# Output projection of a hybrid S5 / HGRN2 layer: sample tokens unsplit on array strips, blocks of every eighth token, two heads split in place, new order lists

## The chip, the cores and the metric

The program runs on one core of one Trainium2 chip. The metric is the device time of one execution in microseconds, as the median of several runs. TensorE (PE) multiplies into PSUM, VectorE (DVE) and ScalarE (ACT) do the elementwise work, GpSimd (POOL) a little of it, and SyncE (SP) issues nearly all DMAs.

## The reference

One layer, 1024 prompt tokens and 32 sample tokens (8 sequences of 4) with states from before. Cut to its core:

```python
h = rmsnorm(x, norm_g); proj = h @ w_in                  # (1056, 1024) @ (1024, 3072)
u, z_s, q, gf, iv, z_h = split(proj, 512 each)
y = S5(u)                                                # 32 groups, complex diagonal state of 64, scan over tokens
g = gelu(y); s5_out = g * sigmoid(g @ w_glu + b_glu) * silu(z_s)
f = lb + (1 - lb) * sigmoid(gf); k = (1 - lb) * sigmoid(-gf)
o = HGRN2(q, k, iv, log f)                               # 4 heads, S_t = diag(f_t) S + k_t v_t', o_t = S_t' q_t
hg_out = rmsnorm_per_head(o) * onorm_g * silu(z_h)
out = concat(s5_out, hg_out) @ w_out                     # (1056, 1024) @ (1024, 1024)
y = rmsnorm(x + out, final_norm_g)                       # also returned: all new states
```

## The kernel before

Every large product is made in float32r from operands split into a high and a low half, as three products: high x high, high x low, low x high. A split is a ScalarE copy (high) and a VectorE subtraction (low). Products of plain f32 tiles run as two records each in the trace.

*Start* (lines 123 to 329): x arrives in tiles of 128 tokens; x_norm takes mean squares (ScalarE, and VectorE for the pairs in DVE_SQ), the root (L172), and scales the tiles (L177, on GpSimd for the pairs in POOL_X, else on VectorE); x_split transposes on TensorE (L188) and splits. Three input projections (L199, tile iu) run as the token chunks come.

*S5 stage* (S5_ORDER): p prepares, m runs the scans of, an eighth of the groups; u, v and z are projections. *Head stage* (H_ORDER): per head f and q are projections, c is the chunkwise recurrence of the 1024 prompt tokens (head_c, two halves), s the sample tokens, n the norm, z the gate's projection, o the transposition and gating (head_out, into tile zh, stored to h_dram); g is an eighth of the GLU, stored to s_dram.

*Output stage* (OUT_ORDER, L990 to L1082): load_a brings one of the eight factors kt (0 to 3 from s_dram, 4 to 7 from h_dram, heads 0 to 3) through a raw buffer, of which there are three, and splits it into ah and al (L1014, L52); factors 0 to 3 are reordered into token order in that pass. load_o does the same for w_out. The 32 sample tokens are split into xs (high and low, 64 columns). Then nine token blocks, the sample block fourth: each takes 2 PSUM banks (the last block three parts) in turn out of eight and accumulates over the factors in the order of OUT_ORDER (L1053; the sample block L1057, two products). Each part is then added to the residual, squared, and the block normalised and stored.

The order lists give the order in which steps are written down and with it their priority; the scheduler of the framework places instructions on each engine's queue by priority and readiness, and the queue then runs in order. Steps under prio() rank above others; issue_after(i) keeps a step behind instruction i on its engine. DMAs that SP issues wait in its queue in order too.

## Time and profile before

| | |
|---|---|
| time, median of 3 runs | 542.88 us (542.69 to 543.5) |
| profiled execution: time, span | 542.94 us, 541.1 us |
| mean granted TensorE clock | 0.993 |
| busy: TensorE, VectorE, ScalarE, GpSimd | 514.6, 386.9, 313.7, 23.7 us |
| share of TensorE in the chain that ended last | 81% |

A row of a timeline gives the start, the time until the end of the group, the engine, the line and the tile names (written <- read). A matmul's duration includes its way through the array; the step from one start to the next is what a stream of them costs. "[2.10 <-ACT KT L805]" says that the engine stood idle for 2.10 us before it and that ScalarE's write of KT ended that.

### The profile page before, as it was taken

The numbers are of one execution on the slowest core, as the hardware profiler recorded it, in microseconds if no ns is written. First come the engines' busy times: TensorE is split into PE (matmuls) and PEld (weight loads), VectorE is DVE, ScalarE is ACT, GpSimd is POOL, SyncE is SP. The second block draws the span as 40 slices with busy tenths as digits, with TensorE's granted clock in tenths as the row PEclk, the third lists the DMA queues.
The fourth block names the chain that finished last, engine by engine and source line by source line (L and its number), as shares of the span: only waits on it lengthen the run. The fifth ranks groups of instructions, "written<-read, shape, count | busy, mean of one in ns | idle before, by whom it ended". The sixth has DMA issues, their size and how long they took to land.

```text
span 541.1 us, 11361 instructions
## 1 busy us (share of the span) xinstructions
PE 514.6 (95%) x4232; PEld 474.4 (88%) x4232; DVE 386.9 (71%) x1075; ACT 313.7 (58%) x877; POOL 23.7 (4%) x79
## 2 busy tenths in 40 slices
PE   2999999999999999999999999999999699999995
PEld 1999999999999999999999999999988577778885
DVE  5897849999989885996569637983699654375233
ACT  5957425645745659553984379835996577333112
POOL 0471000000000100000000000000000000000000
PEclk9999999999999999999999999999999989999999
DMA  8800922341434217333232306343255527535312
GB/s 310 267 20 14 281 59 82 94 150 30 143 130 151 70 64 225 101 102 84 70 95 82 122 9 176 106 122 121 78 149 171 190 84 235 179 125 168 116 40 78
DMA packets 52631, 66.19 MB, mean 122 GB/s; under 512 B 3680, under 2 KB 34272, under 8 KB 52576
## 3 DMA queue, kind: packets, MB, share of 16 engines
q1 hardware_dynamic: 52432, 65.21, 38.0%
q8 instruction: 33, 0.54, 0.4%
q10 hardware_dynamic: 144, 0.26, 0.1%
q14 instruction: 22, 0.18, 0.1%
HBM read 46.43 MB, written 19.02 MB: 121 GB/s over the span
## 4 chain that ended last, share of the span: by engine, by line
PE 81%; ACT 7%; DVE 5%; DMA 3%; issue 2%; SPq 0%; ACTq 0%; DVEq 0%
PE ip L199 32%; PE op L1053 15%; PE vp L253 9%; PE iu L199 7%; PE glu L972 3%; PE xt L188 2%; PE y L572 2%; DMA or<-in_w_out_dram 2%; PE b L516 1%; PE y L574 1%; PE kv L810 1%; DVE Qv L52 1%; DMA wr_b<-in_w_in_dram 1%; ACT S L888 1%; PE po L816 1%
## 5 line engine op out<-in xcount | busy, mean ns | idle before, releaser
L199 PE MATMUL ip<-xh,wl_b 128*128 128x384 f32 (+1 forms) x408 | 133.9, 328 | 0.0
L199 PE MATMUL ip<-xh,wh_b 128*128 128x384 f32 (+1 forms) x408 | 132.9, 326 | 1.0 <-ACT sg L976 0.7
L199 PE MATMUL ip<-xl,wh_b 128*128 128x384 f32 (+1 forms) x408 | 133.3, 327 | 0.0
L199 PEld LDWEIGHTS ip<-xh,wh_b 128*128 128x128 f32 x408 | 76.6, 188 | 1.9 <-ACT sg L976 1.1
L199 PEld LDWEIGHTS ip<-xh,wl_b 128*128 128x128 f32 x408 | 76.9, 188 | 1.0 <-issue 0.6
L199 PEld LDWEIGHTS ip<-xl,wh_b 128*128 128x128 f32 x408 | 76.8, 188 | 0.7 <-issue 0.6
L1053 PE MATMUL op<-oh,ah 128*128 128x512 f32 (+1 forms) x136 | 52.8, 388 | 1.7 <-ACT ah L1014 1.0
L1053 PE MATMUL op<-ol,ah 128*128 128x512 f32 (+1 forms) x136 | 52.1, 383 | 0.0
L1053 PE MATMUL op<-oh,al 128*128 128x512 f32 (+1 forms) x136 | 49.6, 380 | 0.0
L253 PE MATMUL vp<-wh_v,xh 128*128 128x256 f32 x128 | 37.0, 289 | 0.0
L253 PE MATMUL vp<-wh_v,xl 128*128 128x256 f32 x128 | 36.3, 284 | 0.0
L253 PE MATMUL vp<-wl_v,xh 128*128 128x256 f32 x128 | 36.3, 284 | 0.0
L1063 ACT ACTIVATE rsq<-res 128x512 f32<-128x512 f32 (+2 forms) x19 | 11.5, 606 | 39.6 <-DVE res L52 38.6
L104 ACT ACTIVATE wh_b<-wr_b 128x512 fp32r<-128x512 f32 x40 | 24.4, 630 | 15.8 <-DMA wr_b<-in_w_in_dram 11.0
L1053 PEld LDWEIGHTS op<-oh,ah 128*128 128x128 f32 x136 | 26.0, 191 | 7.4 <-ACT ah L1014 1.3
L52 DVE TENSOR_TENSOR res<-op,res 128x512 f32<-128x512 f32 (+2 forms) x19 | 12.3, 660 | 27.2 <-PE op L1053 25.0
L52 DVE TENSOR_TENSOR wl_b<-wr_b,wh_b 128x512 fp32r<-128x512 f32 x40 | 27.3, 684 | 5.5 <-ACT wh_b L104 5.4
L1053 PEld LDWEIGHTS op<-ol,ah 128*128 128x128 f32 x136 | 26.0, 191 | 5.1
L1053 PEld LDWEIGHTS op<-oh,al 128*128 128x128 f32 x136 | 25.7, 190 | 5.2
L199 PE MATMUL iu<-xl,wh_b 128*128 128x256 f32 (+2 forms) x72 | 24.9, 350 | 0.0
L253 PEld LDWEIGHTS vp<-wh_v,xh 128*128 128x128 f32 x128 | 24.2, 189 | 0.4 <-issue 0.4
L253 PEld LDWEIGHTS vp<-wh_v,xl 128*128 128x128 f32 x128 | 24.2, 189 | 0.0
(314 smaller groups left out, 1277.9 us busy)
## 6 DMA issues: line engine op xcount, KB each, us to landing
wr_b<-in_w_in_dram SPq DMA_DIRECT2D x40, 256.0 KB
gr<-y_dram SPq DMA_DIRECT2D x16, 272.0 KB
or<-in_w_out_dram SPq DMA_DIRECT2D x16, 256.0 KB
res<-in_x_p_dram SPq DMA_DIRECT2D x8, 512.0 KB
out_dram<-res SPq DMA_DIRECT2D x7, 512.0 KB
u_dram<-uT SPq DMA_DIRECT2D x4, 576.0 KB
U<-u_dram SPq DMA_DIRECT2D x8, 288.0 KB
y_dram<-Y SPq DMA_DIRECT2D x8, 272.0 KB
```

The costliest lines, as they stand in the source:

```text
L52: eng.tensor_tensor(out=out, in0=a, in1=b, op=op)
L104: S.activation(h, raw, AF.Copy)
L188: PE.transpose(ps[:, n * 128 - n0 : n * 128 - n0 + m], xrs[n][kt // 4][:, kt % 4 * 128 : kt % 4 * 128 + 128], ident[:m, :m])
L199: PE.matmul(ps[:, :nn], a[:, kt * 128 : (kt + 1) * 128], b[kt][:, n0 : n0 + nn], start=(kt == 0 and i == 0), stop=(kt == KT - 1 and i == 2))
L253: PE.matmul(ps[:, :256], a[kt][:, tok], b, start=(kt == 0 and i == 0), stop=(kt == KT - 1 and i == 2))
L516: PE.matmul(ps[:, i * 136 : (i + 1) * 136], W[:, g0 + i, :], U[:, g0 + i, 0:136], start=True, stop=True)
L572: PE.matmul(ps[:, i * 136 : (i + 1) * 136], T[:, g0 + i, :], U[:, g0 + i, 8:144], start=True, stop=False)
L574: PE.matmul(ps[:, i * 136 : (i + 1) * 136], CA[:, g0 + i, 1:9, :].rearrange("p n c -> p (n c)"), SS[:, g0 + i, :], start=False, stop=True)
L810: PE.matmul(pkv[:, sl], KT_[:, sl], v[:, 4 * hb + i, :], start=True, stop=True)
L972: PE.matmul(ps[:, :272], a[:, kt, mo * 128 : mo * 128 + 128], b[:, kt, :], start=(kt == 0 and i == 0), stop=(kt == 3 and i == 2))
L1053: PE.matmul(ps, a[kt][:, tok], b[kt][:, cs], start=(ik == 0 and i == 0), stop=(ik == KT - 1 and i == 2))
L1063: S.activation(sq[:m, cs], r[:m, cs], AF.Square, accum_out=ss[:m, ip : ip + 1])
```

## The change

The 32 sample tokens of the output projection are no longer split: plain f32 products with 32 stationary columns each go to four 32-column strips of the array, four factors at a time, with w_out loaded once more, unsplit; the four partial sums are added on the way out of PSUM, and they are made after blocks 2 and 4. A block of 128 prompt tokens now takes every eighth token, so that factors 0 to 3 are split in the order in which they are stored, while the weights of factors 4 to 7 are read with a step of eight. Heads 2 and 3 are split from their tile zh, with no way through h_dram. In head_c four psC products per group become three. x_norm(0) is written down ahead of the first weights, whose casts go behind its root. Fewer squares go to VectorE and fewer multiplies to GpSimd. fng is loaded after OUT_ORDER into a tile of its own. The output blocks use six banks in turn. The last part's square sums on VectorE, and its scaling is cut in three. The order lists are new. The diff, cut (the old final loop's removed lines are in the listing above):

```diff
-S5_ORDER = "p0 p1 p2 m0 m1 v0 p3 u3 p4 m2 m3 v1 m4 p5 p6 m5 p7 z1 m6 z2 m7 z0 z3"
-
-
-H_ORDER = "f0 q0 c0 s0 g0 z0 g1 f1 q1 c1 n0 s1 g2 o0 z2 f2 n1 g3 q2 c2 g4 z1 s2 n2 o1 g5 f3 g6 q3 c3 s3 o2 n3 g7 z3 o3"
-
-OUT_ORDER = "a0 w5 a1 w1 w0 w2 w4 w3 a5 a3 a4 a2 w6 a6 w7 a7"
+S5_ORDER = "p0 p1 p2 m0 m1 v0 p3 u3 p4 m2 m3 v1 m4 p5 p6 p7 m5 m6 z0 z2 z1 m7 z3"
+H_ORDER = "f0 q0 g0 c0 s0 n0 z0 g1 f1 q1 c1 g2 o0 z2 f2 s1 g4 q2 n1 g3 c2 z1 s2 g5 f3 g6 q3 c3 n2 s3 n3 o2 o1 g7 z3 o3"
+OUT_ORDER = "w5 a1 w2 w0 w1 a0 w4 w3 a5 a3 a4 a2 w6 a6 w7 a7"
 PRIO = 10000
 
-DVE_SQ = {(n, 1) for n in range(5)}
-POOL_X = {(n, 1) for n in range(2, 9)}
+DVE_SQ = {(0, 1), (1, 1)}
+POOL_X = {(n, 1) for n in (5, 6, 7, 8)}
...
             SY.dma_start(raw, src[:, i * 512 : (i + 1) * 512])
-            with prio():
+            with prio(), tc.issue_after(xrs["root"].ins) if name == "b0" else nullcontext():
                 S.activation(h, raw, AF.Copy)
                 tt(V, l, raw, h.bitcast(F32), SUB)
...
-    xs = cp.tile([128, KT, 64], F32R, name="xs")
+    st = cp.tile([128, KT, 32], F32, name="st")
...
         xspare = lambda name: un(name, 576)
+        x_norm(0)
         w0 = load_w(io["w_in"][0], "b0")
...
-                q4 = Qv.rearrange("p (s i e x) -> p s i e x", i=4, e=2, x=hh)
+                last = hh == 32
+                q4 = Qv.rearrange("p (s i e x) -> p s i e x", i=4, e=3 if last else 2, x=hh)
...
-                tt(V, q4[:, :, 0, 1, :], q4[:, :, 3, 0, :], M.unsqueeze(2).to_broadcast([128, ns, hh]), MUL)
+                tt(V, q4[:, :, 1, 2, :] if last else q4[:, :, 0, 1, :], q4[:, :, 3, 0, :], M.unsqueeze(2).to_broadcast([128, ns, hh]), MUL)
...
-                Qn = ht(f"Qv{4 * hh}", 512 if last else 1024)
+                Qn = ht(f"Qv{4 * hh}", 512 if last else 1536 if hh == 8 else 1024)
...
-                q = Q32[:, 256 * n : 256 * n + 256]
+                q = Q32[:, 384 * n : 384 * n + 384]
                 o = 96 * n
-                ks = [K32[:, 128 * n + 32 * j : 128 * n + 32 * j + 32] for j in range(3)]
-                PE.matmul(psC[0:32, o : o + 64], ks[0], q[:, 64:128], start=True, stop=True)
-                PE.matmul(psC[32:64, o : o + 96], ks[1], q[:, 96:192], start=True, stop=True)
-                PE.matmul(psC[64:96, o : o + 96], ks[2], q[:, 128:224], start=True, stop=True)
-                PE.matmul(psC[0:32, o + 64 : o + 96], ks[0], q[:, 32:64], start=True, stop=True)
+                for j, b in enumerate((q[:, 96:192], q[:, 160:256],
+                                       q[:, 96:384].rearrange("p (i x) -> p i x", x=96)[:, :, 0:32])):
+                    PE.matmul(psC[32 * j : 32 * j + 32, o : o + 96],
+                              K32[:, 128 * n + 32 * j : 128 * n + 32 * j + 32], b, start=True, stop=True)
...
-        SY.dma_start(h_dram[h], zg)
+        if h < 2:
+            SY.dma_start(h_dram[h], zg)
...
-    fng = zp.tile([128, NT], F32, name="fng", tag="z", bufs=2)[:, :D]
-    SY.dma_start(fng, io["fng"])
+    fng = fp.tile([128, D], F32, name="fng", bufs=1)
     ahi, alo, ohi, olo = {}, {}, {}, {}
     early = [(wp, "whi", 3, wp, "wlo", 3)] * 2 + [(zp, "v", 4, zp, "v", 4)]
-    st = xs
     def load_a(kt):
         pa, ta, na, pb, tb, nb = early.pop(0) if early else (fp, "a", 10, fp, "a", 10)
         a = pa.tile([128, NP], F32R, name=f"ah{kt}", tag=ta, bufs=na)
         b = pb.tile([128, NP], F32R, name=f"al{kt}", tag=tb, bufs=nb)
-        av = a.rearrange("p (c j) -> p c j", j=8)
-        bv = b.rearrange("p (c j) -> p c j", j=8)
         for i in range(2):
-            src = rawt(f"ar{kt}{i}")
+            half = slice(512 * i, 512 * i + 512)
+            at, bt = a[:, half], b[:, half]
             if kt < 4:
+                src = rawt(f"ar{kt}{i}")
                 SY.dma_start(src, s_dram[kt][:, 544 * i : 544 * i + 544])
                 sj = src.rearrange("p (j t) -> p j t", t=136)
-                pv, qv = sj[:, :, :128].transpose([0, 2, 1]), sj[:, :, 128:].transpose([0, 2, 1])
-                at, bt = av[:, :, 4 * i : 4 * i + 4], bv[:, :, 4 * i : 4 * i + 4]
-                last = i == 0
+                pv, qv = sj[:, :, :128], sj[:, :, 128:].transpose([0, 2, 1])
+                at, bt = (t.rearrange("p (j t) -> p j t", t=128) for t in (at, bt))
+                short = i == 0
             else:
                 n = (512, 544)[i]
-                SY.dma_start(src[:, :n], h_dram[kt - 4][:, 512 * i : 512 * i + n])
-                pv = src[:, :512].rearrange("p (c j) -> p c j", j=8)
-                qv = src[:, 512:544].rearrange("p (c j) -> p c j", j=4)
-                at, bt = av[:, 64 * i : 64 * i + 64], bv[:, 64 * i : 64 * i + 64]
-                last = i == 1
+                if kt < 6:
+                    src = rawt(f"ar{kt}{i}")
+                    SY.dma_start(src[:, :n], h_dram[kt - 4][:, 512 * i : 512 * i + n])
+                else:
+                    src = zgs[kt - 4][:, 512 * i : 512 * i + n]
+                pv = src[:, :512]
+                qv = src[:, 512:n].rearrange("p (c j) -> p c j", j=4)
+                short = i == 1
             S.activation(at, pv, AF.Copy)
             tt(V, bt, pv, at.bitcast(F32), SUB)
-            if last:
-                sh = st[:, kt, 0:32].rearrange("p (c j) -> p c j", j=4)
-                sl = st[:, kt, 32:64].rearrange("p (c j) -> p c j", j=4)
-                S.activation(sh, qv, AF.Copy)
-                tt(V, sl, qv, sh.bitcast(F32), SUB)
+            if short:
+                S.copy(st[:, kt].rearrange("p (c j) -> p c j", j=4), qv)
         ahi[kt], alo[kt] = a, b
+    def tokens(a, kt, n):
+        return a[kt][:, 128 * n : 128 * n + 128] if kt < 4 else a[kt].rearrange("p (c j) -> p j c", j=8)[:, n]
+    def rows(t, n):
+        return t.rearrange("(c j) d -> j c d", j=8)[n]
     def load_o(kt):
         oh = xp.tile([128, NT], F32R, name=f"oh{kt}", tag="x")
...
         for i in range(2):
             cs = slice(512 * i, 512 * i + 512)
             raw = rawt(f"or{kt}{i}")[:, :512]
-            SY.dma_start(raw, io["w_out"][kt][:, cs])
+            xrs["o"] = SY.dma_start(raw, io["w_out"][kt][:, cs])
             S.activation(oh[:, cs], raw, AF.Copy)
             tt(V, ol[:, cs], raw, oh[:, cs].bitcast(F32), SUB)
         ohi[kt], olo[kt] = oh, ol
+    def finish(n, r, sq, ss, ip, cs, parts):
+        m = 128 if n < 8 else 32
+        if n == 7 and ip == 2:
+            V.scalar_tensor_tensor(out=sq[:, cs], in0=r[:, cs], scalar=1.0, in1=r[:, cs], op0=MUL, op1=MUL,
+                                   accum_out=ss[:, 2:3])
+            S.activation(ss[:, 2:3], ss[:, 2:3], AF.Sqrt, bias=ss[:, 3:4], scale=1.0 / D)
+            V.reciprocal(ss[:, 2:3], ss[:, 2:3])
+            S.activation(sq[:, 384:768], r[:, 384:768], AF.Copy, scale=ss[:, 2:3])
+            V.scalar_tensor_tensor(out=sq[:, cs], in0=r[:, cs], scalar=ss[:, 2:3], in1=fng[:, cs], op0=MUL, op1=MUL)
+            V.tensor_scalar(sq[:, 0:384], r[:, 0:384], ss[:, 2:3], None, op0=MUL)
+            SY.dma_start(rows(io["y_p"], n)[:, 0:384], sq[:, 0:384])
+            S.dma_start(rows(io["y_p"], n)[:, 384:D], sq[:, 384:D])
+            return
+        S.activation(sq[:m, cs], r[:m, cs], AF.Square, accum_out=ss[:m, ip : ip + 1])
+        if n == 7:
+            tt(V, r[:, cs], r[:, cs], fng[:, cs], MUL)
+        if ip == 1:
+            tt(V, ss[:m, 0:1], ss[:m, 0:1], ss[:m, 1:2], ADD)
+            V.tensor_scalar(ss[:m, 3:4], ss[:m, 0:1], 1.0 / D, EPS, op0=MUL, op1=ADD)
+        if ip == parts - 1:
+            S.activation(ss[:m, 0:1], ss[:m, 3:4], AF.Sqrt)
+            V.reciprocal(ss[:m, 0:1], ss[:m, 0:1])
+            V.scalar_tensor_tensor(out=r[:m], in0=r[:m], scalar=ss[:m, 0:1], in1=fng[:m], op0=MUL, op1=MUL)
+            SY.dma_start(rows(io["y_p"], n) if n < 8 else io["y_s"], r[:m])
+    def row(n):
+        m = 128 if n < 8 else 32
+        r = fp.tile([128, D], F32, name=f"res{n}", tag="res", bufs=3)
+        SY.dma_start(r[:m], rows(io["x_p"], n) if n < 8 else io["x_s"])
+        sq = fp.tile([128, D], F32, name=f"rsq{n}", tag="rsq", bufs=2)
+        return r, sq, fp.tile([128, 4], F32, name=f"fs{n}", tag="fs", bufs=2)
     emit(OUT_ORDER, {"a": load_a, "w": load_o})
+    SY.dma_start(fng, io["fng"])
     ks = [int(i[1:]) for i in OUT_ORDER.split() if i[0] == "a"]
-    banks, it = (mmt, mmt, mmt, ppt, axt, axt, byt, byt), 0
...
+    banks, it = (mmt, mmt, mmt, axt, axt, byt), 0
+    wfull = [p.tile([128, n], F32, name=f"ws{j}", tag=t, bufs=b)[:, :D]
+            for j, (p, n, t, b) in enumerate(((wp, D, "whi", 3), (wp, D, "wlo", 3), (zp, 1152, "o", 2), (zp, 1152, "o", 2)))]
+    short = []
+    def short_load(i):
+        for j in range(4):
+            SY.dma_start(wfull[j], io["w_out"][ks[4 * i + j]])
+    def short_mms(i):
+        if i == 0:
+            short.extend((ppt("os0"), byt("os1")))
+        for c in range(2):
+            for j in range(4):
+                PE.matmul(short[c][32 * j : 32 * j + 32, :], st[:, ks[4 * i + j], :], wfull[j][:, 512 * c : 512 * c + 512],
+                          start=(i == 0), stop=(i == 1))
+    for n in range(8):
+        r, sq, ss = row(n)
+        parts = ((0, 512), (512, 256), (768, 256)) if n == 7 else ((0, 512), (512, 512))
         for ip, (c0, cn) in enumerate(parts):
             ps = banks[it](f"op{n}{ip}")[:, :cn]
             it = (it + 1) % len(banks)
             cs = slice(c0, c0 + cn)
             for ik, kt in enumerate(ks):
...
+                for i, (a, b) in enumerate(((ahi, ohi), (ahi, olo), (alo, ohi))):
+                    PE.matmul(ps, tokens(a, kt, n), b[kt][:, cs], start=(ik == 0 and i == 0),
+                              stop=(ik == KT - 1 and i == 2))
+            tt(V, r[:, cs], ps, r[:, cs], ADD)
+            finish(n, r, sq, ss, ip, cs, len(parts))
+        if n == 0:
+            with tc.issue_after(xrs["o"].ins):
+                short_load(0)
+        if n == 2:
+            short_mms(0)
+            short_load(1)
+        if n == 4:
+            short_mms(1)
+            r, sq, ss = row(8)
+            for c in range(2):
+                cs = slice(512 * c, 512 * c + 512)
+                tt(V, r[:32, cs], short[c][0:32], r[:32, cs], ADD)
+                for j in range(1, 4):
+                    S.copy(sq[:32, cs], short[c][32 * j : 32 * j + 32])
+                    tt(V, r[:32, cs], r[:32, cs], sq[:32, cs], ADD)
+                finish(8, r, sq, ss, c, cs, 2)
```

## Rows read from the trace of the kernel before

**Rows 1.** The page: busy time, share of the span and instructions by engine.
```profile
PE 514.6 (95%) x4232; PEld 474.4 (88%) x4232; DVE 386.9 (71%) x1075; ACT 313.7 (58%) x877; POOL 23.7 (4%) x79
```

**Rows 2.** Windows: length, busy time of each engine, granted clock, DMA share, GB/s.
```profile
13.50:27.00 13.50, 13.50 (x97) 13.50 (x96) 10.91 (x25) 13.11 (x36) 5.59 (x7) 1.00 0.81 269
397.00:423.00 26.00, 23.92 (x312) 20.84 (x312) 24.92 (x74) 18.64 (x50) 0.00 (x0) 1.00 0.46 151
423.00:441.00 18.00, 13.61 (x127) 11.06 (x127) 10.50 (x31) 10.57 (x32) 0.00 (x0) 0.81 0.50 156
441.00:453.00 12.00, 10.71 (x62) 7.35 (x63) 3.19 (x6) 11.59 (x35) 0.00 (x0) 1.00 0.53 177
```

**Rows 3.** Waits of TensorE: us in total, times, longest.
```profile
PE xt L188 <- DVE xr L177: 10.0, 1, 10.0
...
PE kt L803 <- DVE C L791: 1.5, 1, 1.5
...
PE op L1053 <- ACT ah L1014: 1.0, 1, 1.0
```

**Rows 4.** Timeline of the start: start us, us, engine, line, tile, shape [idle before].
```profile
6.60 0.15 DVE L170 SCALAR_TENSOR_TENSOR rstd<-ss_x 128x2 f32<-128x2 f32 x1
...
8.02 0.19 ACT L172 ACTIVATE rstd<-rstd 128x2 f32<-128x2 f32 x1
...
8.76 0.16 DVE L173 RECIPROCAL rstd<-rstd 128x2 f32<-128x2 f32 x1
...
9.42 1.67 DVE L177 TENSOR_SCALAR xr<-xr,rstd 128x512 f32<-128x512 f32 x4
...
15.47 5.11 POOL L177 TENSOR_SCALAR xr<-xr,rstd 128x512 f32<-128x512 f32 x3 [13.79 <-DVE rstd L173]
```

**Rows 5.** Chain pieces (start, us, what), then two timeline rows of TensorE.
```profile
243.82 0.89 PE kv L810 x8
...
265.47 0.57 PE oS L880 x16
...
445.43 0.39 PE L1057 MATMUL op<-ol,xs 128*64 128x512 f32 x1
...
448.66 0.40 PE L1057 MATMUL op<-ol,xs 128*64 128x512 f32 x1
```

**Rows 6.** Timeline of TensorE: first and last of one sC group.
```profile
427.88 0.24 PE L771 MATMUL sC<-Qv,K 128*32 128x64 f32 x1 [0.49 <-ACT o L823]
...
428.54 0.23 PE L774 MATMUL sC<-Qv,K 128*32 128x32 f32 x2
```

**Rows 7.** Output passage: durations (min/median/max ns), timelines, a wait of SP, chain.
```profile
L1014 ACT ACTIVATE ah<-ar x16: 614/841/1212, 396.4 to 473.5; 128x512 fp32r<-128x512 f32 x16
...
L52 DVE TENSOR_TENSOR al<-ar,ah x16: 680/860/1143, 397.6 to 474.2; 128x512 fp32r<-128x512 f32 x16
...
396.43 1.14 ACT L1014 ACTIVATE ah<-ar 128x512 fp32r<-128x512 f32 x1
...
426.07 1.28 ACT L1030 ACTIVATE oh<-or 128x512 fp32r<-128x512 f32 x2 [4.19 <-DMA or<-in_w_out_dram]
...
SPq L989 <- DMA h_dram<-zh: 2.8, 1, 2.8
...
433.04 2.08 PE L810 MATMUL kv<-v,KT 128*128 128x128 f32 x8 [2.10 <-ACT KT L805]
...
435.11 3.35 PE op L1053 x9
```

**Rows 8.** Weight loads of two lines: ns min/median/max, first and last start, shape.
```profile
L1053 PEld LDWEIGHTS op<-oh,ah x136: 186/188/333, 418.8 to 534.8; 128*128 128x128 f32 x136
...
L880 PEld LDWEIGHTS oS<-S,Qm x64: 106/110/110, 265.4 to 441.5; 128*32 128x32 f32 x64
```

**Rows 9.** Timeline of the close.
```profile
535.44 0.42 DVE L52 TENSOR_TENSOR res<-op,res 128x256 f32<-128x256 f32 x1 [1.16 <-PE op L1053]
...
537.73 0.37 ACTq L1077 DMA_DIRECT2D out_dram<-rsq  x1
```

More of the change, by code (lines that the diff above doesn't have):

```diff
@@ L1 @@
 import math
-from contextlib import ExitStack
+from contextlib import ExitStack, nullcontext
 import concourse.bass as bass
@@ L1037, in hybrid_layer @@
-    for n in (0, 1, 2, 8, 3, 4, 5, 6, 7):
-        m = 128 if n < 8 else 32
-        tok = slice(n * 128, n * 128 + 128)
-        r = fp.tile([128, D], F32, name=f"res{n}", tag="res", bufs=3)
-        SY.dma_start(r[:m], io["x_p"][tok] if n < 8 else io["x_s"])
-        sq = fp.tile([128, D], F32, name=f"rsq{n}", tag="rsq", bufs=2)
-        ss = fp.tile([128, 4], F32, name=f"fs{n}", tag="fs", bufs=2)
-        last = n == 7
-        parts = ((0, 512), (512, 256), (768, 256)) if last else ((0, 512), (512, 512))
+    banks, it = (mmt, mmt, mmt, axt, axt, byt), 0
@@ L1050, in hybrid_layer @@
             for ik, kt in enumerate(ks):
-                if n < 8:
-                    for i, (a, b) in enumerate(((ahi, ohi), (ahi, olo), (alo, ohi))):
-                        PE.matmul(ps, a[kt][:, tok], b[kt][:, cs], start=(ik == 0 and i == 0),
-                                  stop=(ik == KT - 1 and i == 2))
-                else:
-                    for i, b in enumerate((ohi, olo)):
-                        PE.matmul(ps[:64], st[:, kt, :], b[kt][:, cs], start=(ik == 0 and i == 0),
-                                  stop=(ik == KT - 1 and i == 1))
```

30 lines of the change are left out of this document (3 added, 27 removed).

## The prediction

> **What bounds the kernel now.** I read the page's engine table first, then the busy time by stretch, then what TensorE waited for, and last the timelines of the stretches in which it waited. TensorE is busy for 514.6 of 541.1 us [rows 1], so 26.5 us are left in which no matmul is under way. Three places hold most of it: the first 10.0 us until the first transposition has a normalised x tile [rows 3]; the stretch from 397 to 453 us, where the three windows leave 2.1, 4.4 and 1.3 us, 7.8 together [rows 2]; and the close after the last matmul, from about 535.4 to 541.1, 5.7 us [rows 9]. That leaves 3.0 us for everything else. So a change pays if it takes TensorE work out, or shortens one of these three; work taken from another engine pays only inside them. The middle stretch costs more than its idle time: in 423 to 441 the granted clock is 0.81 [rows 2], and behind an idle 2.10 us the eight kv records took 2.08 us, where another head's take 0.89, and the nine output matmuls behind them took 3.35 us, where nine steps of 0.231 are 2.1 [rows 5, 7]: 1.2 and 1.3, 2.5 us lost to the lower clock. The stretch could give back 10.3 us at most. Behind 453 us nothing of this kind is left: output matmuls follow each other at one pitch and the waits list nothing later.
>
> **Part 1, the start.** Before, the root of block 0's mean squares is issued on ScalarE behind a weight cast. Its operand is there at 6.60 + 0.15, but it runs at 8.02, its reciprocal at 8.76, and the multiplies of x begin at 9.42, behind two low-half subtractions of the same weight [rows 4]. After, x_norm(0) is emitted first and the casts of "b0" go behind the root. The chain becomes 6.75 + 0.19 + 0.16, so the multiplies can begin at about 7.1: 2.3 us earlier, and TensorE with them. Against it: three squares of x tiles 2 to 4 go from VectorE to ScalarE, which is busy 13.11 of 13.50 us in the next window; a 512-wide ScalarE pass costs at least 0.61 [rows 2, 7], so up to 1.8 us come later there. For it: three multiplies leave GpSimd, where they took 5.11 us in a row [rows 4], for VectorE, which is busy 10.91 of 13.50. The low halves of the first weight come up to 1.67 us later, behind the multiplies; they are needed last of the three products, and high halves cover that. Bounds -2.3 and +0.5; I take -1.8, near the first, since VectorE and GpSimd shorten together.
>
> **Part 2, one matmul fewer of four in head_c (psC).** One group of 32 records runs from 427.88 to the last start at 428.54 plus its 0.23, 0.89 us [rows 6]. After there are 24 records; 64 + 32 columns on strip 0 become one of 96, so the strips stream the same columns and only the records' own cost falls. If all went by records: 8 / 32 of 0.89, 0.22, times 8 groups, 1.8 us; if by columns, nothing. I take -0.6, nearer the columns. The wider Qv32 tile changes no count of VectorE work.
>
> **Part 3, the 32 sample tokens.** Before: 32 matmuls of 512 columns with 64 stationary columns. Fourteen steps from 445.43 to 448.66 are 0.231 us each [rows 5], so 7.4 us of TensorE. After: 16 unsplit products of 512 columns, two records each like every f32 matmul here, 32 records, on four 32-column strips. A record of 128 f32 columns on the whole array costs 0.89 / 8 = 0.111 us, so 0.445 at 512 columns; four strips at once make 32 x 0.445 / 4 = 3.6 us. Four strips do run at once in this trace: sixteen oS records of 128 columns, each strip with its own moving data, take 0.57 us up to the next matmul, 36 ns each [rows 5]; scaled to 512 columns that is 4.6 us, fill included. I take 4.2: -3.2 (bounds -3.8 and -2.8). It also drops the lower half of the token split. Its new 8 x 512 KB of w_out are about 4.2 MB over four blocks of 48 x 0.231 = 11 us, under 100 GB/s beside the 151 to 177 of the busiest stretch, at half of the DMA engines' time [rows 2]: priced at nothing. These loads stand on SP's queue and wait for the last projection's weight buffers and for head 3's tile; behind them wait residual loads and stores of y. A late residual holds two of six PSUM banks; two further blocks, 22 us of matmuls, cover that. The evacuation (six copies, eight adds) lies beside them.
>
> **Part 4, the passage from the heads to the output projection.** Four edits act on the 397 to 453 stretch. (a) Factors 0 to 3 are split without reordering: the ScalarE pass now takes from 0.61 to 1.21 us and VectorE's from 0.68 to 1.14 [rows 7], and the slow ones are those that reorder; eight of each save about 0.5 and 0.4, four of them while VectorE is busy 24.92 of 26.00 us [rows 2]. (b) Heads 2 and 3 are split in place: two stores, four loads and four raw buffers of a ring of three go. (c) The load of fng no longer stands before w_out's loads on SP: it waited 2.8 us there for a store of zh [rows 7], and the cast of w_out behind it then waited 4.19 us on ScalarE, whose queue held the KT copy that TensorE waited 2.10 us for [rows 7]. (d) The order lists. (c) and (b) attack the stalls of 2.1 and, through buffers, 1.5 [rows 3], the slow clock (2.5) and the 1.0 for ah: 7.1. Against it: the output blocks turn in six banks instead of eight, so one fewer block is open while factors are missing; and o1 now stands after o2, while factor 5 (head 1) is still third in every accumulation and still goes through DRAM. I charge 2 for that: -5.0, between 0 and -10.3. The moves of gates and heads further up can only touch the 3.0 us left over: 0, within 2 either way.
>
> **Part 5, every eighth token.** For factors 0 to 3 the stationary 128 columns stay contiguous; for 4 to 7 they are read with a step of eight elements. No weight load of the trace does that. A contiguous load lasts 188 ns for 128 columns and 110 for 32 [rows 8]: 0.81 ns a column, 104 for 128, hidden behind the 231 of a 512-column matmul. The nearest stepped access is ScalarE's reordering pass: 1.14 against 0.61 us over 512 elements [rows 7] is 1.04 ns more for each. With that, 128 columns load in 104 + 133 = 237 ns. There are 180 stepped loads with 512 columns to hide behind, which would pay 0.006 each, and 24 in the last block with 256 columns, 0.117 if half of 512 and a little (0.231 / 2), which would pay 0.12: 1.1 + 2.9 = 4.0 us. Bounds 0 and +4.0 (the rival goes further); a load only reads, where the pass reads and writes with a step, so I take half, +2.0. The residual and output rows stay 4 KB each: nothing.
> [...]
>
> **Part 6, the close.** From the last add at 535.44 to the second store at 537.73 [rows 9] the square's accumulation moves to VectorE and the scaling is cut in three; steps of nearly the same length replace others: -0.1.
>
> **Sum.** -1.8 - 0.6 - 3.2 - 5.0 + 2.0 - 0.1 = -8.7. The profiled run took 542.94 us (span 541.1 and 1.8 around it), which makes 534.2; the median is 542.88, so that stands: 534.2.
>
> **The rivals.** *The passage keeps its stalls:* six banks and a late factor 5 make new waits of the size of the old ones: 534.2 + 5 = 539.2. For it: ScalarE is busy 11.59 of 12.00 us in 441 to 453 [rows 2], with the norms now bunched there. Against: fng and four raw buffers are gone. *The passage is cleared:* all 10.3, and 2.3 at the start: 534.2 - 5.3 - 0.5 = 528.4. *The strips do not run at once at 512 columns:* 32 x 0.445 = 14.2 us, 6.8 more than before instead of 3.2 less: 534.2 + 10 = 544.2, at the edge of slower. Against it stands the oS row. *The stepped weight loads bind:* Here the load becomes the bound in place of the stream. The cost is 180 x (L - 0.231) + 24 x (L - 0.117). It decides from L of about 0.28 us, 2.7 times the contiguous load: there 8.8 + 3.9 = 12.7 us stand against 10.7 of gains, and it is 545, slower. At 0.30 it is 549, at four times the load (0.416) 33.3 + 7.2 = 40.5 and 573.
>
> **Chances.** Forecast 0.53, stalls kept 0.20, cleared 0.12, strips in series 0.05, loads binding 0.10. A range of 527 to 543 leaves out the binding loads, the strips in series and a little below. About 0.2% (1.1 us) is what a measurement tells from no change; part of the kept stalls and of the strips fall there: faster 0.82, same 0.06, slower 0.12.
>
> **What would show it.** First transposition near 7.7 us instead of 9.96; eight strip records of 512 columns starting within about 1 us, 16 in 2; 24 sC records; no wait of SP for a zh store and no 4 us wait of ScalarE for w_out; fewer than 5 us of TensorE idle between 390 and 450 and no slow clock there; equal pitch of the matmuls of factors 0 to 3 and 4 to 7, also in the 256-column parts, where 117 ns against 237 settles part 5. The prediction is wrong if the pitch of the last blocks rises, or if TensorE waits for factor 5 or a bank.

## The result and the profile after

The changed kernel takes 547.25 us (median of 4 runs, 546.98 to 547.66) against 542.79 before: 1.0084 times, interval 1.0067 to 1.0102. Slower by 4.5 us where 8.7 less were forecast. The profiled spans are 545.2 and 541.1.

The page's engine table of the changed kernel, to be read beside [rows 1]:

```profile
PE 516.3 (95%) x4168; PEld 483.0 (89%) x4168; DVE 383.1 (70%) x1070; ACT 313.9 (58%) x885; POOL 18.7 (3%) x76
```

There are 64 matmul records fewer, and yet TensorE is busy 1.7 us longer and its weight loads 8.6 us longer. The four windows of [rows 2]:

```profile
13.50:27.00 13.50, 12.85 (x94) 12.21 (x93) 10.51 (x25) 13.22 (x37) 0.41 (x2) 1.00 0.80 274
397.00:423.00 26.00, 23.80 (x344) 21.47 (x330) 23.20 (x74) 18.07 (x53) 0.00 (x0) 1.00 0.52 160
423.00:441.00 18.00, 13.46 (x73) 11.33 (x74) 10.67 (x29) 11.94 (x38) 0.00 (x0) 0.72 0.49 160
441.00:453.00 12.00, 10.93 (x61) 8.96 (x52) 3.96 (x7) 9.29 (x28) 0.00 (x0) 1.00 0.63 220
```

The passage from the heads to the output projection (397 to 453 us) holds as much idle time as before (2.2, 4.5 and 1.1 us against 2.1, 4.4 and 1.3), and its clock in 423 to 441 is lower: 0.72 against 0.81. The waits of TensorE behind it, to be read beside [rows 3]:

```profile
PE xt L189 <- DVE xr L178: 7.7, 1, 7.7
PE kt L805 <- DVE C L793: 2.7, 1, 2.7
...
PE op L1107 <- ACT ah L1019: 2.1, 2, 1.1
PE kv L812 <- ACT KT L807: 1.9, 1, 1.9
```

The start came as forecast: the first transposition stands at 7.7 instead of 10.0 us. The wait for C grew from 1.5 to 2.7 and the one for a factor from 1.0 to 2.1.

The weight loads of the output matmuls (min/median/max ns, first and last start, shape), then the timeline of TensorE in the last block, where the matmuls have 256 columns. Beside [rows 8]:

```profile
L1107 PEld LDWEIGHTS op<-oh,ah x136: 186/316/365, 432.6 to 538.5; 128*128 128x128 f32 x136
...
531.12 0.28 PE L1107 MATMUL op<-oh,ah 128*128 128x256 f32 x1
531.24 0.28 PE L1107 MATMUL op<-ol,ah 128*128 128x256 f32 x1
531.35 0.29 PE L1107 MATMUL op<-oh,al 128*128 128x256 f32 x1
531.48 0.40 PE L1107 MATMUL op<-oh,ah 128*128 128x256 f32 x1
531.71 0.41 PE L1107 MATMUL op<-ol,ah 128*128 128x256 f32 x1
531.96 0.40 PE L1107 MATMUL op<-oh,al 128*128 128x256 f32 x1
532.19 0.28 PE L1107 MATMUL op<-oh,ah 128*128 128x256 f32 x1
532.31 0.28 PE L1107 MATMUL op<-ol,ah 128*128 128x256 f32 x1
```

The first three and the last two belong to factors 0 to 3, with contiguous tokens: a step of 0.117 us. The three from 531.48 belong to a factor of 4 to 7, with every eighth token: a step of 0.24. (The median of 316 ns above is taken over contiguous and stepped loads together; singly, the contiguous loads of this trace last about 0.19 us and the stepped ones 0.32 to 0.34, on average 0.33.) With 512 columns the same view shows these steps:

```profile
474.15 0.41 PE L1107 MATMUL op<-oh,al 128*128 128x512 f32 x1
474.39 0.41 PE L1107 MATMUL op<-oh,ah 128*128 128x512 f32 x1
474.64 0.41 PE L1107 MATMUL op<-ol,ah 128*128 128x512 f32 x1
474.89 0.40 PE L1107 MATMUL op<-oh,al 128*128 128x512 f32 x1
475.21 1.93 PE L1095 MATMUL os<-ws,st 128*32 128x512 f32 x16
477.07 0.50 PE L1107 MATMUL op<-oh,ah 128*128 128x512 f32 x1
477.41 0.39 PE L1107 MATMUL op<-ol,ah 128*128 128x512 f32 x1
477.64 0.39 PE L1107 MATMUL op<-oh,al 128*128 128x512 f32 x1
```

Ahead of the strips the step is 0.2445 on average (factors 4 to 7), behind them 0.2295 (factors 0 to 3). The strips themselves work: sixteen records of 512 columns go by in 1.86 us, 3.7 for all, where the 32 matmuls before took 7.4 [rows 5].

The close is as long as before: the last add stands 5.6 us ahead of the end, against 5.7 [rows 9].

```profile
539.58 0.42 DVE L52 TENSOR_TENSOR res<-op,res 128x256 f32<-128x256 f32 x1 [2.62 <-PE op L1107]
```

Counted at 460 us: before, 285 output matmuls of 512 columns, 48 of 256 and 16 of the sample tokens are left, 71.0 + 3.7 = 74.7 us at the contiguous steps; after, 278, 48 and the strips, 69.4 + 3.7 = 73.1. So the gains forecast ahead of 460 us, 10.6 us (start, psC, strips, passage), have shrunk to 1.6, and the stepped loads come on top.

### The profile page after: what moved, and what is told of

Its sections match the earlier page's. It is cut to its first block, busy times and chain, and to the rows that moved or that the text cites. A ratio compares the mean times of both kernels' runs of the same rounds, so it can differ in the third digit from the quotient of the medians.

```text
span 545.2 us, 11241 instructions
## 1 busy us (share of the span) xinstructions
PE 516.3 (95%) x4168; PEld 483.0 (89%) x4168; DVE 383.1 (70%) x1070; ACT 313.9 (58%) x885; POOL 18.7 (3%) x76
## 4 chain that ended last, share of the span: by engine, by line
PE 76%; DVE 9%; DMA 8%; ACT 4%; issue 2%; SPq 0%; DVEq 0%; ACTq 0%
PE ip L200 28%; PE op L1107 17%; PE vp L254 7%; PE iu L200 6%; PE glu L975 3%; DVE Qv L52 2%; DMA or<-in_w_out_dram 2%; DMA wr_b<-in_w_in_dram 2%; PE y L574 1%; PE y L576 1%; PE b L518 1%; PE po L818 1%; DMA s_dram<-zg 1%; PE xt L189 1%; DMA xr<-in_x_p_dram 1%
## 5 line engine op out<-in xcount | busy, mean ns | idle before, releaser
L200 PE MATMUL ip<-xh,wl_b 128*128 128x384 f32 (+1 forms) x408 | 132.2, 324 | 0.0
L1107 PE MATMUL op<-oh,ah 128*128 128x512 f32 (+1 forms) x136 | 54.1, 404 | 2.1 <-ACT ah L1019 2.1
L1107 PE MATMUL op<-ol,ah 128*128 128x512 f32 (+1 forms) x136 | 53.8, 397 | 0.0
L1107 PE MATMUL op<-oh,al 128*128 128x512 f32 (+1 forms) x136 | 52.1, 399 | 0.0
L1107 PEld LDWEIGHTS op<-oh,ah 128*128 128x128 f32 x136 | 35.2, 262 | 6.8 <-ACT ah L1019 2.5
L1107 PEld LDWEIGHTS op<-ol,ah 128*128 128x128 f32 x136 | 35.5, 262 | 2.4
L1107 PEld LDWEIGHTS op<-oh,al 128*128 128x128 f32 x136 | 35.1, 261 | 2.8
L52 DVE TENSOR_TENSOR res<-op,res 128x512 f32<-128x512 f32 (+1 forms) x17 | 11.0, 659 | 35.2 <-PE op L1107 24.3
L200 PE MATMUL iu<-xh,wh_b 128*128 128x256 f32 (+2 forms) x72 | 23.8, 338 | 1.2 <-ACT xh L191 0.9
```

What stands on the lines that cost most here:

```text
L52: eng.tensor_tensor(out=out, in0=a, in1=b, op=op)
L200: PE.matmul(ps[:, :nn], a[:, kt * 128 : (kt + 1) * 128], b[kt][:, n0 : n0 + nn], start=(kt == 0 and i == 0), stop=(kt == KT - 1 and i == 2))
L1107: PE.matmul(ps, tokens(a, kt, n), b[kt][:, cs], start=(ik == 0 and i == 0), stop=(ik == KT - 1 and i == 2))
```

## The experiments

All kernels are compared with the kernel before on the same chip in the same comparison; ratios are to it. The changed kernel's own is 1.0084.

### Contiguous loads, old lists, the start alone

**e1_contig**: the changed kernel; factors 4 to 7 are reordered by ScalarE and VectorE as before, so that all weight loads are contiguous.

```
-  pv = src[:, :512]
+  pv = src[:, :512].rearrange("p (c j) -> p c j", j=8)
+  at, bt = (t.rearrange("p (j c) -> p c j", j=8)[:, 64*i : 64*i+64] for t in (a, b))
-  return a[kt][:, 128*n : 128*n+128] if kt < 4 else a[kt].rearrange("p (c j) -> p j c", j=8)[:, n]
+  return a[kt][:, 128*n : 128*n+128]
```

> The changed kernel with factors 4 to 7 also stored in block order when they are split, so that every weight load is contiguous; the pass that splits them writes with a step instead. TensorE's order of instructions is that of the changed kernel. Theory (stepped weight loads bind): the step from matmul to matmul of factors 4 to 7 falls from 0.2445 to 0.23 us at 512 columns (180 of them, 2.7 us) and from 0.241 to 0.118 at 256 columns (24 of them, 2.95 us): 547.25 - 5.65 = 541.6, up to 1 us more if the slower passes lengthen the stalls between 410 and 460 us. Rival (the blocks are slower because w_out and the strided rows are loaded beside them): the steps stay and the time stays at 547.

Measured: 540.87 us, 0.9974 (0.9959 to 0.9989). 1.1% or 6.0 us come off the changed kernel by this edit alone, and every step is the contiguous one again. The weight loads and the 256-column step of this kernel:

```profile
L1108 PEld LDWEIGHTS op<-oh,ah x136: 186/188/365, 433.3 to 534.0; 128*128 128x128 f32 x136
...
528.79 0.28 PE L1108 MATMUL op<-oh,ah 128*128 128x256 f32 x1
528.91 0.28 PE L1108 MATMUL op<-ol,ah 128*128 128x256 f32 x1
```

**e2_oldlists**: the changed kernel with the three order lists of before. **e7_contig_oldlists**: both edits.

> The changed kernel with the three order lists of the kernel before. Theory (the lists put no output matmul ahead of the second half of head 3 on TensorE's queue, so that TensorE stands idle while that half's casts and DMAs come): 18 output matmuls stand there again, the stretch from 410 to 440 us gives back about 4 us and the middle of the kernel 1 to 2: 547.25 - 5.5, between 540.5 and 543.5. Rival (six banks instead of eight, heads split in place and fng's late load make the stall): it stays, 546 to 547.5.

> Both edits: contiguous weight loads and the three lists of the kernel before, everything else as changed. Theory: the two add up, 547.25 - 5.65 - 5.5 = 536, between 534.5 and 538: faster than the kernel before by the short products (3.2) and the start (2). Rival (the gains share one stretch and overlap): 540 to 542.

Measured: 545.04 us, 1.0053 (1.0032 to 1.0074), and 540.26 us, 0.9962 (0.9946 to 0.9979). e2 lies between its two theories, e7 in the range of its rival (the gains overlap). The new lists cost about 1.7 us beside stepped loads (the intervals just overlap) and hardly anything without (0.6 us, not clear of noise). With both undone, the 5.6 us forecast for start, psC and strips leave 2.1.

**e4_start**: the kernel before with the start's edits alone (the norm of block 0 ahead of the first weight, the first weight's casts behind its root, fewer squares and multiplies moved).

> The kernel before with the start's edits alone: the first normalisation ahead of the first weights, their casts behind its root, squares and multiplies moved. Theory: first transposition at 7.7 instead of 10.0 us and 2 us of it kept to the end: 542.8 - 2.0 = 540.8. Rival (ScalarE, with three squares more, or the scans in 100 to 200 us, which VectorE bounds, give it back): 542.5 to 543.

Measured: 541.56 us, 0.9996 (0.9978 to 1.0014). The 1.8 us are not seen at the end: the interval allows a gain of 1.2 us at most. The two traces have the same lists and show where the lead goes. The first transposition stands 2.1 us ahead of the kernel before, the last matmul of iu (56.8 us) 1.1, and the first of glu (223.5) less than 0.1.

### Parts alone, and filling the idle time

**e8_strips**: the kernel before with the strips alone, six banks. **e9_inplace**: the kernel before with heads 2 and 3 split in place and fng in its own buffer.

```
 e8:  -  banks = (mmt, mmt, mmt, ppt, axt, axt, byt, byt)        # and 32 matmuls of xs
      +  banks = (mmt, mmt, mmt, axt, axt, byt)                  # and 16 short products of st
 e9:  -  src = rawt(f"ar{kt}{i}")                               # and its load from h_dram
      +  src = rawt(f"ar{kt}{i}") if kt < 6 else zgs[kt - 4][:, 512 * i :]
```

> The kernel before (542.4 us in the last comparison) with one part of the change alone: the 32 sample tokens go through the unsplit short products on four strips, their weights loaded again, six PSUM banks instead of eight for the rest. Theory 1: 7.4 us of TensorE time become 3.7 and the rest of 0.5 us goes to the extra loads and adds: 539.0 to 539.8 us. Theory 2: two banks fewer and the extra loads cost what is gained, in the passage from the heads to the projection: 541.5 to 543 us.

> The kernel before (542.4 us in the last comparison) with one part alone: the outputs of heads 2 and 3 are split where they stand, without a store to memory and a load back, and the final norm's row has a buffer of its own. Theory 1 (the prediction's): the store and load and the held buffer cause the stalls of the passage, and this takes about 5 us: 537 to 538.5 us. Theory 2: the stalls are head 3's chain of transposes, copies and state products, which stays; only what TensorE has in its queue between them counts, and that grows by 6 products: 540.8 to 542 us. Theory 3: no difference, 542 to 543 us.

Measured: 543.07 us, 1.0027 (1.0010 to 1.0043), and 539.93 us, 0.9960 (0.9945 to 0.9975). The strips alone lose, although their records are short. Where e8's TensorE stood still behind 460 us, and its first strips:

```profile
463.61 0.50 PE L1068 MATMUL op<-oh,ah 128*128 128x512 f32 x1 [1.48 <-ACT ah L1014]
...
468.78 1.90 PE L1048 MATMUL os<-ws,st 128*32 128x512 f32 x4 [0.74 <-DMA ws<-in_w_out_dram]
471.30 0.51 PE L1068 MATMUL op<-oh,ah 128*128 128x512 f32 x1 [0.61 <-ACT ah L1014]
...
475.65 1.93 PE L1048 MATMUL os<-ws,st 128*32 128x512 f32 x12
```

With six banks open, the first output matmul that needs the seventh factor is the 109th (6 x 6 x 3 = 108 come ahead of it), and the first that needs the eighth is the 127th (6 x 7 x 3 = 126). TensorE waits 1.48 us for the one and, behind the 126th at 467.6 and the first strip, 0.61 for the other; with eight banks they would be the 145th and the 169th. It also waits 0.74 for the reloaded weights. And the first strip's four records ran alone: they took 1.90 us, as long as the twelve of the other three strips later, so that these sixteen records cost 1.9 us more than in the changed kernel. So the strips pay with the banks that they take, and in this order of instructions with a strip that runs by itself. In e7, where heads 2 and 3 are split in place, neither the 109th nor the 127th waits and the strips run together. Splitting in place is worth 0.4% alone, 2 us, not 5.

One more thing goes with the strips. In the kernel before, 16 matmuls of the sample tokens, 3.7 us, ran from 445.15 us on [rows 5], ahead of a factor for which TensorE then waited until 452.6. The change moves this work behind blocks 2 and 4. No run separates that from the loss of the two banks.

**e5_o1**: e1 with head 1's output step earlier in the list (o1 ahead of q3). What it goes by is the trace of the changed kernel, where that step comes late, the first output matmul starts at 432.7 us (418.8 before), and TensorE is busy for 3.78 of the 10 us in 420 to 430 at a granted clock of 0.72 (8.28 at 1.00 before). **e10_cover**: e7 with 27 output matmuls placed by hand in the gaps of head 3; for this the first loads of the projection and head 2's output step (o2) come ahead of head 3's second half.

```
 e10: +  done = cover(0)                          # 9 output matmuls, traced ahead of sC
      +  with tc.issue_after(done.ins): ...       # sC; then 9 more, kt, 9 more, kv
```

> The changed kernel with contiguous weight loads (540.9 us when measured so, span of its profile 540.3), its new lists kept but for one item: the output step of head 1 stands before the last head's query block instead of three places later. [...] With the step earlier 18 products stand ahead of head 3's second half and 9 between its transposes and its state products: 536 to 538.5 us, TensorE busy over 8 of the 10 us in 420 to 430. Theory 2: head 3's own chain on VectorE and ScalarE sets the time of this stretch and filled slots on TensorE are paid again later: 540 to 541.5 us.

> The changed kernel with contiguous weight loads and the old lists (540.3 us, span 538.1) and one more edit: the first three loads of activations and of weights of the output projection are issued ahead of head 3's second half, and 27 products of the output projection (three banks, three of the eight factors) are placed by hand: 9 before the last level's score products, 9 between these and the key transposes, 9 between the transposes and the state products. Theory 1: the two waits of 1.5 to 2.5 us there and the fall of the clock are what is left of the passage's stall; each 9 products cover 2.1 us: 535 to 537.5 us. Theory 2: the loads' casts ahead of head 3's vector work make its chain later by as much: 539.5 to 541 us.

Measured: 542.91 us, 1.0021 (1.0003 to 1.0039), and 540.09 us, 0.9971 (0.9951 to 0.9992). The gain was forecast at 536 to 538.5 us in e5 and at 535 to 537.5 in e10, and came in neither. In e10 the wait for KT (2.5 us in e7) is gone and the clock was higher (median of the runs 0.996 against 0.992 in e7), but a wait of 2.1 us ahead of sC has come, and the end did not move. What did not change either is seen in the timelines of TensorE, e7 first, then e10 (idle before, and its releaser, in brackets):

```profile
449.60 0.50 PE L1108 MATMUL op<-oh,ah 128*128 128x512 f32 x1 [1.58 <-ACT ah L1020]
...
456.12 0.50 PE L1108 MATMUL op<-oh,ah 128*128 128x512 f32 x1 [1.50 <-ACT st L1023]
```

```profile
449.28 0.50 PE L1057 MATMUL op<-oh,ah 128*128 128x512 f32 x1 [1.15 <-ACT ah L1024]
...
455.90 0.50 PE L1057 MATMUL op<-oh,ah 128*128 128x512 f32 x1 [1.59 <-ACT st L1027]
```

Counted in the order of the output matmuls, these are the 55th and the 73rd in both kernels: six banks times three or four ready factors times three matmuls are 54 and 72, and the next one needs a factor that isn't there. The same count for the changed kernel and the five like it (six banks, three factors in early buffers):

| kernel | 55th (us) | 73rd (us) | span | span - 73rd |
|---|---|---|---|---|
| after | 451.3 | 457.4 | 545.2 | 87.8 |
| e2 | 449.8 | 455.9 | 543.7 | 87.8 |
| e1 | 451.8 | 458.4 | 540.3 | 81.9 |
| e5 | 454.3 | 459.7 | 541.7 | 82.0 |
| e7 | 449.6 | 456.1 | 538.1 | 82.0 |
| e10 | 449.3 | 455.9 | 538.5 | 82.6 |

From the 73rd on it is a fixed length: 82 to 83 us with contiguous loads and 87.8 with stepped ones (the difference, 5 to 6 us, is the price of the step once more). What TensorE saves or loses ahead of that point, by stalls or by the clock, counts only as far as the point moves, and e10 did not move it (455.9 against 456.1). In e5 TensorE waited 6.0 us for C, in two waits, and reached it later.

### More matmuls ahead of the wall

All on e7. **e11_early4**: a fourth factor in buffers that are free early. **e12_banks8**: eight banks for the first eight products, the strips two blocks later. **e13_both**, and **e14_all** with e10's placing too.

```
 e11: +  early = [(wp, "whi", 3, wp, "wlo", 3)] * 2 + [(zp, "v", 4, zp, "v", 4), (wp, "whi", 3, wp, "wlo", 3)]
      +  OUT_ORDER = "a0 w5 a1 w1 w0 w4 a5 a4 w2 w3 a3 a2 w6 a6 w7 a7"      # ws0 and ws1 go to fp
 e12: +  banks = (mmt, mmt, mmt, ppt, axt, axt, byt, byt, mmt, mmt, mmt, axt, axt, byt, mmt, mmt, mmt)
      +  short_mms(0) behind block 4, short_mms(1) behind block 5
```

> The changed kernel with contiguous weight loads and the old lists (540.3 us) with four factors of the output projection instead of three in buffers that are free before the heads end (the fourth, head 0's, takes the weight buffers that the sample tokens' reloaded weights had, and these go to the projection's own pool). Theory 1 (a wall): in every kernel with six PSUM banks the 55th matmul of the projection is the first that needs the fourth factor, and it starts at 449 to 454 us whatever was done ahead, because that factor's buffer and its pass on ScalarE come behind head 3's norm; six banks times three factors times three matmuls are 54. With four factors it is the 73rd, so up to 18 x 0.23 = 4.1 us of TensorE's work move ahead of the wall: 536 to 537.8 us. Theory 2: ScalarE, busy 9.6 of 10 us in 440 to 450, sets the stretch and the idle time only moves: 539.5 to 541 us.

> The same kernel as the base of the last (contiguous loads, old lists, 540.3 us), three early factors, but eight PSUM banks instead of six for the first eight products of the output projection; the sample tokens' strips, which hold two of the banks, come two blocks of tokens later. Theory 1 (a wall at banks times ready factors): the 73rd matmul is the first that needs the fourth factor; up to 4.1 us move ahead of the wall: 536 to 537.8 us. Theory 2: 539.5 to 541 us.

> Both edits at once, on the same base: eight banks and four early factors, 96 matmuls ahead of the wall. Theory 1: TensorE stood idle or slow for some 10 us in 420 to 456 us of the base, and has matmuls for 9.6 us more: the rest of the stall goes but for what head 3's own chain and the clock cost: 533.5 to 536 us. Theory 2: 539.5 to 541 us.

> Both edits and the 27 products placed by hand ahead of and between head 3's last steps (540.1 us when these were tried alone). Theory 1: placing them alone gave nothing because the same 54 matmuls ran earlier and TensorE then waited longer at the wall (55th matmul at 449.3 us against 449.6 without); with 96 ahead of the wall it pays: 532.5 to 535 us, at or below the run with both edits alone. Theory 2: 539.5 to 541 us.

Measured: 542.18 us, 1.0005 (0.9984 to 1.0025); 538.11 us, 0.9927 (0.9899 to 0.9956); 539.59 us, 0.9961 (0.9941 to 0.9980); 539.13 us, 0.9948 (0.9925 to 0.9971). Two banks more, with the strips two blocks later, pay 0.35%, about 1.9 us, half of the bound (the intervals of e7 and e12 overlap a little; e17 against e18 below, in one comparison, gives 0.6% clear of noise). The fourth early factor pays nothing, but not because of a wall: in e11 the 73rd matmul, now the first that needs the fifth factor, comes at 455.2 without a wait, and e13 waits at no such place either. What their traces show instead lies ahead of it. The matmuls had been used up early, TensorE waited 1.2, 0.4 and 1.7 us for head 3's own steps in e11 (1.3, 0.5 and 1.0 in e13), and the clock fell: 0.66 in 440 to 450 in e11, 0.72 in e13, where e7 ran at 1.00. In e11 a strip ran alone again besides (twelve records, then four), which is 1.9 of the 2.3 us between e11 and e7. So matmuls moved ahead of a wall left a gap where they had been; that this is all of it was not tried.

### What holds the fifth factor

**e15_scale**: e7 with head 3's nine scaling copies on VectorE. **e16_st**: e7 with the in-place heads' sample copies on GpSimd. **e18_scale_st**: both. **e17_best**: both on e12.

```
 e15: -  S.activation(ov[:m, n, :], ov[:m, n, :], AF.Copy, scale=ss[:m, n : n + 1])
      +  V.tensor_scalar(ov[:m, n, :], ov[:m, n, :], ss[:m, n : n + 1], None, op0=MUL)   # h == 3
 e16: -  S.copy(st[:, kt].rearrange("p (c j) -> p c j", j=4), qv)
      +  (G.tensor_copy if kt >= 6 else S.copy)(st[:, kt].rearrange("p (c j) -> p c j", j=4), qv)
```

> The changed kernel with contiguous loads and the old lists (540.3 us), head 3's nine scaling copies moved from ScalarE (2.74 us, 446.3 to 449.0) to VectorE, which is idle then. Theory 1 (the wall is ScalarE's queue): the fourth factor's pass starts when the table load and the root end (446.0) instead of 449.0, the 55th matmul comes at about 447 instead of 449.6, and the time falls by about as much where the next wall does not take it back: 537.5 to 539 us. Theory 2: the wall is elsewhere (the clock, TensorE): 540 to 541 us.

> The same base, one edit: the two copies of the sample tokens of the heads split in place go to GpSimd. In the base ScalarE's queue stands 3.8 us (451.1 to 454.9) at such a copy, which waits for head 3's last product, while the passes over other factors stand behind it; the 73rd matmul waits for one of these until 456.1. Theory 1: this second wall goes, 1 to 1.6 us: 538.7 to 539.4 us. Theory 2: no difference, 540 to 540.8 us.

> Both of these edits on the same base, six banks. Theory 1: both walls move, 55th matmul at about 447 and none waiting after it: 536 to 538 us. Theory 2: 540 to 541 us.

> Both edits and eight banks for the first eight products (538.1 us with the banks alone). Theory 1: more matmuls ahead of walls that come sooner: 535 to 537.5 us. Theory 2: with eight banks the walls are no longer reached first, and the two edits give nothing: 538 to 539 us.

Measured: 541.75 us, 0.9992 (0.9971 to 1.0013); 540.95 us, 0.9983 (0.9964 to 1.0003); 541.49 us, 0.9992 (0.9967 to 1.0017); 538.17 us, 0.9933 (0.9914 to 0.9952). No gain in any; three of them are even 0.2 to 0.3% above e7's ratio, which stays unexplained (the intervals touch or overlap). What held the fifth factor in the changed kernel is seen in ScalarE's timeline, and then in the chain that ended last:

```profile
456.64 0.22 ACT L1022 COPY st<-zh 128x32 f32<-128x32 f32 x1 [4.30 <-DVE zh L52]
```

```profile
454.81 1.40 PE op L1107 x6
456.21 0.19 PE ot L939
...
456.42 0.20 DVE zh L52
...
456.64 0.22 ACT st L1022
456.86 0.54 ACT ah L1019
```

ScalarE stood 4.30 us at the copy of the sample tokens of a head that is split in place, and the pass over the fifth factor (ah) stood behind it in the queue. The copy needed a tile whose transposition (ot) stood on TensorE's queue behind the output matmuls of the fourth factor. In e7 the copy stood 3.8 us, until 454.9. e16 and e18 take it off ScalarE, and now the pass waits for its transfer, until 456.0 in e16 and 456.3 in e18. So two things held the fifth factor until nearly the same time, and taking one away gives nothing.

In e18 the 55th matmul came 1 us sooner than in e7 (448.7), the 73rd not (457.4). SP's queue and a piece of the chain of waits of e18:

```profile
444.90 1.40 SPq L1082 DMA_DIRECT2D fng<-in_fng_dram  x1
446.34 2.42 SPq L1077 DMA_DIRECT2D res<-in_x_p_dram  x3
449.64 0.33 SPq L1016 DMA_DIRECT2D ar<-h_dram  x1
...
449.64 6.66 DMA ar<-h_dram
```

The second half of the fifth factor, 272 KB, is on its way for 6.66 us, behind 2 MB issued just ahead of it: the final norm's row and three residual loads of 512 KB each. In the kernel before the row had gone earlier, the three residual loads stood there too, and this load was issued at 452.67, 3.1 us behind the last of them; its pass on ScalarE began at 455.42.

**e19_res**: e18 with the row and the residual loads issued after the last load of a factor. **e20_best2**: the same on e17.

```
+  with tc.issue_after(xrs["a"].ins):        # the last load of a factor from s_dram
       SY.dma_start(fng, io["fng"])          # and the residual loads in row()
```

> The last six-bank kernel (contiguous loads, old lists, head 3's scaling on VectorE, copies of the sample tokens on GpSimd: 541.5 us) with the final norm's row and the residual loads issued after the last load of a factor. Theory 1 (the fifth factor's load is queued behind 2 MB): it lands about 3 us sooner, the 73rd matmul comes at 452 to 454 instead of 457.4, and the time falls by 2 to 4 us: 537.5 to 539.5 us. Theory 2: the transfers are not what holds it: 540.5 to 542 us.

> The same edit on the kernel with eight banks for the first eight products (538.2 us), whose TensorE lost only 1.1 us in 440 to 460: little is left to gain there. Theory 1: 537 to 538 us. Theory 2: 538 to 538.6 us, or worse if the residuals now come late for the first blocks.

Measured: 538.90 us, 0.9935 (0.9914 to 0.9956), and 537.44 us, 0.9923 (0.9904 to 0.9942). SP's queue and the same piece of the chain in e19:

```profile
450.77 0.33 SPq L1016 DMA_DIRECT2D ar<-h_dram  x1
451.49 1.81 SPq L1007 DMA_DIRECT2D ar<-s_dram  x2
453.40 0.38 SPq L1084 DMA_DIRECT2D fng<-in_fng_dram  x1
453.83 0.90 SPq L1078 DMA_DIRECT2D res<-in_x_p_dram  x2
...
450.77 2.77 DMA ar<-h_dram
```

The load now takes 2.77 us, the 73rd matmul comes at 454.7 and none of the output matmuls waits any more in 440 to 460; 0.57% come off e18 by moving four loads, and the intervals are apart. Against e7, whose ScalarE still has the copy and the scaling, it is 0.27%, and the intervals overlap. So the wall was the copy, and right behind it a queue of transfers. The four loads were moved together: what the row alone costs is not shown, and the move was not tried without the edits of e15 and e16. With eight banks the wall was nearly out of reach already, and the move gives 0.1%, within the intervals. e20 is the fastest of all, 0.8% under the kernel before and 1.6% under the changed one.

## Why the prediction was wrong

**Stepped weight loads (part 5): the step that turned the sign.** The estimate of the load was nearly right: 0.33 us beside 0.19 is some 0.14 more, so by its own working 104 + 141 = 245 ns where 237 stood, and the measured steps, 0.2445 and 0.241, agree with that estimate. What failed was "I take half, +2.0", argued from a load that only reads, against the only row that bore on it. The price at 256 columns was right (0.123 paid, 0.12 forecast, 24 times: 2.95). At 512 columns 0.006 became 0.015 (0.2445 against 0.2295, 180 times: 2.7): there the estimate of the load (237 ns, 245 with the measured 0.14 us) lies just above the stream (231), so that a few ns more of it double the price. Together 5.65, above the upper bound of 4.0; e1 takes it away and the time falls by 6.0. The rival "stepped loads bind" needed loads of 0.28 us to come out slower; 0.245 were enough, because other gains were missing too.

**The passage (part 4): -5.0 forecast; start, psC and passage together -7.4 forecast, +2.1 measured** (the lead of 1.6 us at 460 less the 3.7 of the strips). Four things were wrong in it.

- The step "(c) and (b) attack the stalls" treated the stalls of the passage as if each microsecond filled were one gained. They stand ahead of a wall: banks times ready factors times three matmuls. e10 took the wait of 2.5 us for KT away, the wall stayed where it was, and nothing was gained.
- "One fewer block is open while factors are missing", with 2 us charged, was the right thought as a lump. Counted out, six banks allow 54 and 72 matmuls of prompt tokens where eight allow 72 and 96; e12 shows what that is worth (1.9 us, 3.2 by e17 against e18). In the kernel before two of the eight held the sample tokens, whose 3.7 us of cover were not counted as lost.
- Edit (b), splitting in place, was priced as transfers and buffers saved. That its copy of the sample tokens goes into ScalarE's queue ahead of the fifth factor's pass was not followed: in the changed kernel ScalarE stood 4.30 us there.
- Of the moved load of fng I priced only the place that it left (w_out's loads). The place where it went, ahead of the fifth factor's load and together with the residuals, was never costed. e19 against e18 shows the price of that whole queue once the copy is gone, 2.7 us at the 73rd matmul.

That is nearly the rival "the passage keeps its stalls": six banks and a late factor. It named factor 5 (head 1's) as the late one; it was the fifth in order, factor 4 (head 0's). With its 5.0 us and the stepped loads at their full price it gives 534.2 + 5.0 + 3.65 = 542.9; of the 4.4 us left to 547.25 the next two points hold some 3.3, and the rest is open.

**The start (part 1): -1.8 forecast, and reached at 7.7 us, but not at the end.** Alone (e4) it is worth 0.2 us, give or take 1. The prediction ended the step where the transpositions begin; where the lead is spent further on was not followed. In e4 half of it is gone by 57 us and all of it by 224; at which wait was not tried by an experiment.

**The lists: 0 within 2.** With stepped loads they cost about 1.7 us (e2, not quite clear of noise), inside the bound. The reason read from the trace, head 1's late step, was tried (e5) and is wrong: with that step earlier the ratio is 1.0021, in e1 0.9974.

**Strips (part 3): right in TensorE's time,** 3.7 us instead of 7.4 (3.2 less were forecast). The 4.2 MB of reloaded weights did not disturb the changed kernel; in e8 TensorE waited 0.7 us for them. **psC: too large:** a group went from 0.885 to 0.861 us, some 0.2 for all eight instead of 0.6. **Close: right.**

Of the signs named beforehand, the steps of factors 4 to 7 and the slow clock in the passage (0.72) were the two that told at once.

## What to carry to other kernels

Count what an engine can have in hand before it must wait (open accumulators times ready operands, here 54 and 72 matmuls), and find the wait that comes last: idle time filled ahead of it was worth nothing in e10, where it did not move (455.9 us against 456.1), and two things can hold it at once, as the copy and the transfer did here. A small copy that waits can hold a large pass: ScalarE stood 4.30 us at one of 32 columns, with the fifth factor's pass behind it. A load that is moved out of one queue's way must be priced at the place where it arrives, with what stands behind it there (272 KB in 6.66 us instead of 2.77). Where one row bears on an unknown cost, take its price and not half of it (237 ns by the row, 241 to 245 measured).

## What the runs showed of the hardware

- In the changed kernel, loading 128 stationary f32 columns with a step of eight elements (32 bytes) took about 0.14 us more than contiguous ones (0.33 against 0.19 in the profile); behind a 512-column matmul the step grew from 0.2295 to 0.2445 us, behind a 256-column one from 0.117 to 0.241.
- Four strips of 32 columns, each with its own 512 moving columns, ran at once in the changed kernel: sixteen records in 1.86 us. Four records of one strip by itself took 1.90 (e8).
- 272 KB landed in 2.77 us (e19), or in 6.66 us behind 2 MB issued from 4.7 us before it on (e18).
- The mean granted clock differed between executions of one kernel, and in e18 the time mostly with it: 538.6 and 538.8 us at 0.995, 540.9, 542.1 and 544.9 at 0.987. In the changed kernel the 10 us behind a stretch in which TensorE stood idle for 2.43 of 4 us had a mean granted clock of 0.52, and 512-column output matmuls at their end (433.24 to 434.52 us) followed each other at 0.43 us instead of 0.23:

```profile
420.00:424.00 4.00, 1.57 (x28) 1.08 (x27) 3.53 (x11) 3.02 (x10) 0.00 (x0) 1.00 0.63 174
424.00:434.00 10.00, 6.21 (x26) 5.35 (x27) 8.76 (x22) 6.87 (x20) 0.00 (x0) 0.52 0.63 210
```
